# A hybrid decoder layer on one core: DeltaNet keys transposed on TensorE instead of through VectorE and DRAM, norm factors stored by GpSimd, head 0's values turned later

## The chip, the cores and the metric

The kernel runs on one core of a Trainium2 chip. The metric is the device time of one execution in microseconds, taken as the median of several executions. A profile is a record of one execution; it names TensorE as PE (its weight loads as PEld), VectorE as DVE, ScalarE as ACT, GpSimd as POOL and SyncE, which issues DMAs, as SP.

## The reference

Two decoder layers on 512 tokens of 1024 columns, float32. Each layer runs two branches side by side on the same normalised input, merges them with gates, projects the result, and adds a feed-forward block. What the change touches is the DeltaNet branch with its 8 heads of 128 columns, cut to its core:

```python
q, k, v, z, beta, decay = parts of  rmsnorm(x) @ w_in
q, k, v = silu(causal_conv4(q | k | v));  q, k = l2norm(q) * 128**-0.5, l2norm(k)
# per head, in chunks, with g the running sum of log decay in a chunk:
L      = strict_lower((k * beta) @ k.T * decay)           # I + L is inverted against
u, w   = solve(I + L, v * beta),  solve(I + L, k * beta * exp(g))
for each chunk, with a state S of 128 x 128:
    v_new = u - w @ S
    o     = (q * exp(g)) @ S + (q @ k.T * decay) @ v_new
    S     = S * exp(g_last) + (k * exp(g_last - g)).T @ v_new
o = rmsnorm(o, norm_g) * silu(z)                          # per head and token
```

The layer then forms sigmoid(gate_a) * (o @ w_up_dn) + sigmoid(gate_b) * (swa @ w_up_sw), projects it with w_o, and adds the feed-forward block. swa is a sliding-window attention with sinks.

## The kernel before, in words

**Tiling.** Activations lie with columns on the 128 partitions and the 512 tokens along the free side. A float32 matmul is made of three faster ones on high and low halves, so a projection of 128 columns (`mm_a`) is 8 x 3 = 24 matmuls of 128x128 by 128x512. Weights come in as `wr`, ScalarE makes the high half `wh`, VectorE the low half `wl`. The chunk of the delta rule is 128 tokens here, so a head has 4 chunks (`NC`).

**Stages of a layer.** First norm and projections, mixed with the sliding-window attention. There the keys of all heads are made and stored to DRAM (`kkd`), as are the decay matrices (`dd`), and a triangular solve (`solve`) prepares blocks of the inverse. Then a loop over eight blocks (`ps_us`, m = 0..7) up-projects the attention branch; ahead of it `d_dense(0)` makes head 0's values, queries and gate. Then the DeltaNet stage, a loop over 8 heads. In head h it calls, in this order:

- `d_keys(h + 1)`: loads `D` and `kk`, forms the factor `kds`, and makes `kd`, the keys with tokens on the partitions, times that factor;
- `d_inverse(h)`: three levels of the block inverse for heads h .. h + 3 (`ps_i` on TensorE, small copies on VectorE; on GpSimd a MEMSET and copies into `Pt`, then two copies into `T`);
- `d_chain(h)`: `ps_qk` and `aT`, then per chunk `ps_ks`, `rr`, `ps_y`, `yy`, `ps_su`, the state `St`, and `ps_o`; each step waits for the one before it, and what is left of TensorE is filled with the projections of the next head;
- `d_step`: one step of the norm of a finished head (`d_tail`, three steps that are spread over later heads). The sums of squares go to DRAM as a row (`sd`), come back as 128x4 (`ff`), GpSimd raises them to the power −1/2, they go to DRAM again (`fd`) and come back on all partitions (`fb`), and VectorE multiplies `yf` with them;
- `d_dense(h + 1)`: the projections `ps_vp`, `ps_qp`, `ps_zp` of the next head, 24 matmuls each, with a convolution of three VectorE operations on values and on queries.

After the last head come the remaining gate projections (`ps_ga`), `yT` (the halves of `yf`), the up-projection `ps_ud`, w_o and the feed-forward block.

**How keys and values get their tokens onto the partitions.** `by_token` does both. VectorE transposes 32x32 blocks of a 128x512 tile (STREAM_TRANSPOSE), four DMAs store the result to DRAM with the blocks in their new places (`kxd` or `vxd`), and one DMA loads it back (second half of the tile `kx` or `vx`). Keys of all heads share one tile `kx`, values one tile `vx`. ScalarE then makes four scaled copies of 128x128 each (`kd`, `vs`).

**What sets the order.** The program text gives priorities; a scheduler then lays out each engine's instructions in one fixed queue, and each engine works through its queue in order, waiting where an input is late. All dynamic DMAs are issued by SP, in its own order. PSUM banks come from pools: two for projections (`PM`), three for the chain (`PS`), one for `ps_i` (`PK`), and two (`PZ`, tag "ss") for a second `ps_i` tile and `ps_o`.

Of the kernel before, what the change touches and what calls it, by code (L numbers as in the profile page):

```python
# [10 lines left out]
F32 = mybir.dt.float32  # L11
# [3 lines left out]
AF = mybir.ActivationFunctionType  # L15
# [5 lines left out]
P = 128  # L21
# [4 lines left out]
H = 8  # L26
# [93 lines left out]
def hybrid_trunk(ctx, tc, x, positions, pre_mix_g, dn_conv_w, dn_a_log, dn_dt_bias, dn_norm_g,  # L120
# [15 lines left out]
    act, stt = nc.scalar.activation, nc.vector.scalar_tensor_tensor  # L136
    tt, ts = nc.vector.tensor_tensor, nc.vector.tensor_scalar
    ptt = nc.gpsimd.tensor_tensor
    dma = nc.sync.dma_start

    def pool_of(tag, bufs):
        def get(name, dt=F32, n=512):
# [112 lines left out]
    pd = dr.tile([P, 1024], F32, name="pd")  # L255
    dd = dr.tile([H, P, 512], F32, name="dd")
    kkd = dr.tile([H, P, 512], F32, name="kkd")
    kxd = dr.tile([H, P, 512], F32, name="kxd")
    vxd = dr.tile([H, P, 512], F32, name="vxd")
    gd = dr.tile([32, P], F32, name="gd")  # L260
    sd = dr.tile([H, 512], F32, name="sd")
# [258 lines left out]
    for l in range(depth):  # L520
# [460 lines left out]
        dn = {}  # L981

        urs = [X4("ur") for i in range(2)]
        kx, vx = X4("kx"), X4("vx")
        uview = lambda h: c4(urs[h // 2 % 2][:, h % 2 * 512:(h % 2 + 1) * 512])
        lo_, hi_ = slice(0, 64), slice(64, 128)
        r0, r1, r2, r3 = (slice(b * 32, (b + 1) * 32) for b in range(4))
# [68 lines left out]
                    ts(out=c4(Pt)[ra, :, rb], in0=v4(psq[ra, 256:384]), scalar1=-1.0, scalar2=None,  # L1056
                       op0=ALU.mult)

        def by_token(src, x_, via):


            a_, b_ = x_[:, 0:512], x_[:, 512:1024]
            nc.vector.transpose(a_.rearrange("p (b c i) -> p b c i", b=4, c=NC),
                                src.rearrange("p (c b j) -> p b c j", b=4, c=NC))
            for a in range(4):
                dma(via[:, a * P:(a + 1) * P].rearrange("(b j) f -> j b f", b=4),
                    a_[a * 32:(a + 1) * 32, :].rearrange("j (b f) -> j b f", b=4))
            dma(b_, via)
            return b_.rearrange("p (a c i) -> p a c i", a=4, c=NC)

        def d_keys(h):

            d, k_ = T[3]("D"), T[3]("kk")
            dma(d, dd[h])
            dma(k_, kkd[h])
            kds = sm.tile([P, NC], F32, name="kds")
            tc.keep_in_program_order(tt(out=kds, in0=cj[h], in1=c4(d)[:, :, P - 1], op=ALU.mult))
            kt = by_token(k_, kx, kxd[h])
            kd = T[7]("kd")
            for c in range(NC):  # L1080
                act(out=kd[:, c * P:(c + 1) * P].rearrange("p (a i) -> p a i", a=4), in_=kt[:, :, c, :],
                    func=AF.Copy, scale=kds[:, c:c + 1])
            dn["k", h] = d, k_, kd

        def d_dense(h, after=lambda: None):
            egb = T[6]("egb")
            dma(c4(egb), egd[h * NC:(h + 1) * NC, :].partition_broadcast(P))
            ps = PM("ps_vp")
            mm_a(ps, hT)
            vt = by_token(conv_silu(ps, 16 + h, T[5], "vv"), vx, vxd[h])  # L1090
            after()
            ps = PM("ps_qp")
            mm_a(ps, hT)
            qq = conv_silu(ps, h, T[4], "qq")
            after()
            ps = PM("ps_zp")
            mm_a(ps, hT)
            sz = T[6]("sz")
            act(out=sz, in_=ps, func=AF.Tanh, scale=0.5)
            stt(out=sz, in0=sz, scalar=1.0, in1=ps, op0=ALU.add, op1=ALU.mult)  # L1100
            after()
            d_step(h - 2)
            qe = T[7]("qe")
            ptt(out=qe, in0=qq, in1=egb, op=ALU.mult)

            wq = T[4]("wq")
            act(out=wq, in_=qq, func=AF.Square, scale=(EPS * P) ** 0.5)
            dn["d", h] = qq, qe, wq, vt, sz

        yf = []  # L1110

        def d_tail(h):

            w, y1 = dn.pop(("t", h))
            wh, wl = pair(T[5], "w")
            split(w, wh, wl)
            ps = PS("ps_w")
            mm(ps, lhsT=ones_r, rhs=wh, start=True, stop=False)
            mm(ps, lhsT=ones_r, rhs=wl, start=False, stop=True)
            nc.scalar.copy(w[0:1], ps[0:1])  # L1120
            dma(sd[h:h + 1, :], w[0:1])
            yield
            ff = sm.tile([P, NC], F32, name="ff")
            dma(ff, sd[h, :].rearrange("(p j) -> p j", p=P))
            ptt(out=ff, in0=ff, in1=mhalf, op=ALU.pow)
            dma(fd[h, :].rearrange("(p j) -> p j", p=P), ff)
            yield
            fb = T[6]("fb")
            dma(fb, fd[h, :].partition_broadcast(P))
            tt(out=y1, in0=y1, in1=fb, op=ALU.mult)  # L1130
# [8 lines left out]
        def d_chain(h):  # L1139
            Pt = dn.pop(("p", h))  # L1140
            d, k_, kd = dn.pop(("k", h))
            qq, qe, wq, vt, sz = dn.pop(("d", h))
            ps = PS("ps_qk")
            for c in range(NC):
                sl = slice(c * P, (c + 1) * P)
# [5 lines left out]
                    op0=ALU.mult, op1=ALU.mult)  # L1151
            vs = US("vs")
            for c in range(NC):
                act(out=vs[:, c * P:(c + 1) * P].rearrange("p (a i) -> p a i", a=4), in_=vt[:, :, c, :],
                    func=AF.Copy, scale=irk[h][:, c:c + 1])
            po = PZ("ps_o")
            St = None
            for c in range(NC):
# [35 lines left out]
        for t in range(NT):  # L1194
            tsl = slice(t * P, (t + 1) * P)
            for g in range(2):
                for j in range(g * 4, g * 4 + 4):
                    hi, lo = oT[j]
                    split(qt[t][:, j * P:(j + 1) * P], hi[:, tsl], lo[:, tsl])
        d_dense(0, lambda: steps(2))  # L1200
        for m in range(KT):
            ps = PM("ps_us")
            mm_a(ps, oT)
            mb = T[7]("mb")
            stt(out=mb, in0=sgb[m], scalar=1.0, in1=ps, op0=ALU.add, op1=ALU.mult)
            dma(mbd[m], mb)
            steps(2 if m < 6 else 40)
        for m in range(NA, NA2):
            ga_early(m)

# [238 lines left out]
```

## Time and profile before

| | us |
|---|---|
| median of 3 executions | 1840.2 (1839.76 to 1841.08) |
| the profiled execution's own time | 1841.73 |
| its span from first to last instruction | 1839.7 |
| TensorE busy | 1811.6 |
| VectorE busy | 1297.1 |
| ScalarE busy | 942.2 |
| GpSimd busy | 211.3 |

The mean granted clock of TensorE is 0.998 of full speed. The DeltaNet stage lies at about 291 to 490 us (layer 0) and 1198 to 1414 us (layer 1) of the span.

A row of the time line reads: start, duration, engine, line of the kernel, operation, output tile, inputs, shapes, count, and in brackets the time that the engine stood idle before it and what ended that. Two matmuls overlap: the second starts before the first has drained, so the time that a matmul costs TensorE is read from one start to the next (0.23 us between full ones), not from its duration (0.39). The same line numbers are used in the whole text; they are those of the kernel before, and in the pieces of the changed order those of the changed kernel, which differ by a few.

A row of the view by stretches reads: from:to in us, length, then busy us and instructions of PE, PEld, DVE, ACT and POOL, the granted clock of TensorE as a share, the share of the DMA engines, and GB/s.

### The profile page before, as it was taken

The page shows a single profiled execution, that of the slowest core. Times are in us where ns is not written, and L with a number is a line of the kernel's source. Part 1 is how long each engine was busy: PE and PEld are TensorE (multiplying, and loading weights), DVE is VectorE, ACT ScalarE, POOL GpSimd, SP SyncE. Part 2 cuts the span into 40 slices and gives each one's busy share as a digit, 9 for nine tenths or more (in the row PEclk, how much of TensorE's full clock was granted, in tenths as well). Part 3 has the DMA queues.
Part 4 walks back from the last instruction along what each step waited for, and adds up shares of the span by engine and source line. Part 5 has one row for each costly group of instructions (what it writes and reads, how often), then busy time and mean ns, then how long its engine had stood idle before and what let it go on. Part 6 is the DMA issues. An engine that isn't in the chain of part 4 may idle for free.

```text
span 1839.7 us, 26716 instructions
## 1 busy us (share of the span) xinstructions
PE 1811.6 (98%) x9598; PEld 1504.2 (82%) x9598; DVE 1297.1 (71%) x2466; ACT 942.2 (51%) x1913; POOL 211.3 (11%) x370
## 2 busy tenths in 40 slices
PE   9999999999999999999999999999999999999998
PEld 7888788778788888888898887887787888888886
DVE  5499796888566668684556987878784667585934
ACT  6678743444334645554347877234343346554542
POOL 0322101221101000000013231022111010000000
PEclk9999999999999999999999999999999999999999
DMA  5533447565453263464245333575555533544631
GB/s 187 201 117 117 115 134 228 159 172 162 118 200 126 92 217 121 167 218 149 93 155 179 113 118 104 172 212 160 151 160 155 170 116 124 185 153 152 229 107 46
DMA packets 148214, 278.48 MB, mean 151 GB/s; under 512 B 35361, under 2 KB 68449, under 8 KB 148082
## 3 DMA queue, kind: packets, MB, share of 16 engines
q1 hardware_dynamic: 148082, 276.79, 47.0%
q8 instruction: 75, 1.23, 0.3%
q14 instruction: 57, 0.47, 0.1%
HBM read 239.38 MB, written 37.36 MB: 150 GB/s over the span
## 4 chain that ended last, share of the span: by engine, by line
PE 79%; DVE 7%; ACT 5%; DMA 4%; issue 3%; POOL 1%; SPq 0%; POOLq 0%; DVEq 0%; ACTq 0%
PE ps_f L340 6%; PE ps_f L339 6%; PE ps_f L341 5%; PE ps_p L402 4%; PE ps_p L404 3%; PE ps_p L400 3%; PE ps_b L388 3%; PE ps_b L387 3%; PE ps_b L389 2%; PE ps_us L339 2%; PE ps_us L340 2%; PE ps_us L341 2%; PE ps_qp L340 2%; PE ps_qp L341 1%; PE ps_qp L339 1%
## 5 line engine op out<-in xcount | busy, mean ns | idle before, releaser
L323 ACT CAST wh<-wr 128x1024 fp32r<-128x1024 f32 (+1 forms) x332 | 343.4, 1040 | 557.6 <-PE ps_f L340 145.9
L324 DVE TENSOR_TENSOR wl<-wr,wh 128x1024 fp32r<-128x1024 f32 (+1 forms) x332 | 398.8, 1211 | 304.7 <-ACT wh L323 301.3
L339 PE MATMUL ps_f<-g_h,wh 128*128 128x512 f32 x448 | 174.3, 389 | 0.0
L340 PE MATMUL ps_f<-g_l,wh 128*128 128x512 f32 x448 | 174.3, 389 | 0.0
L341 PE MATMUL ps_f<-g_h,wl 128*128 128x512 f32 x448 | 174.3, 389 | 0.0
L402 PE MATMUL ps_p<-wl,P_h 128*128 128x512 f32 x336 | 131.3, 391 | 0.8 <-DVE wl L324 0.8
L404 PE MATMUL ps_p<-wh,P_l 128*128 128x512 f32 x336 | 130.8, 389 | 0.0
L400 PE MATMUL ps_p<-wh,P_h 128*128 128x512 f32 x336 | 129.5, 389 | 0.0
L437 POOL TENSOR_TENSOR pr<-pq,pw 128x1 f32<-128x1 f32 x16 | 9.7, 608 | 804.1 <-DVE pq L436 804.1
L341 PEld LDWEIGHTS ps_f<-g_h,wl 128*128 128x128 f32 x448 | 84.1, 188 | 17.5
L339 PEld LDWEIGHTS ps_f<-g_h,wh 128*128 128x128 f32 x448 | 84.1, 188 | 17.5
L340 PEld LDWEIGHTS ps_f<-g_l,wh 128*128 128x128 f32 x448 | 84.1, 188 | 17.2
L402 PEld LDWEIGHTS ps_p<-wl,P_h 128*128 128x128 f32 x336 | 63.1, 188 | 15.5 <-DVE wl L324 2.2
L400 PEld LDWEIGHTS ps_p<-wh,P_h 128*128 128x128 f32 x336 | 63.1, 188 | 13.3
L404 PEld LDWEIGHTS ps_p<-wh,P_l 128*128 128x128 f32 x336 | 63.1, 188 | 12.8
L387 PE MATMUL ps_b<-wh,h_h 128*128 128x432 f32 (+1 forms) x192 | 71.1, 370 | 0.0
L388 PE MATMUL ps_b<-wl,h_h 128*128 128x432 f32 (+1 forms) x192 | 70.6, 368 | 0.2 <-DVE wl L324 0.2
L389 PE MATMUL ps_b<-wh,h_l 128*128 128x432 f32 (+1 forms) x192 | 70.3, 366 | 0.0
L293 DVE TENSOR_TENSOR wr<-wr 128x1024 f32<-128x1024 f32 x48 | 57.9, 1219 | 2.5 <-DMA wr<-in_weights_dram 1.9
L339 PE MATMUL ps_qp<-h_h,wh 128*128 128x512 f32 x128 | 54.2, 424 | 0.0
L341 PE MATMUL ps_qp<-h_h,wl 128*128 128x512 f32 x128 | 53.4, 417 | 0.0
L340 PE MATMUL ps_qp<-h_l,wh 128*128 128x512 f32 x128 | 53.2, 416 | 0.0
(358 smaller groups left out, 4874.3 us busy)
## 6 DMA issues: line engine op xcount, KB each, us to landing
wr<-in_weights_dram SPq DMA_DIRECT2D x320, 512.0 KB, 4.1
wr<-in_weights_dram SPq DMA_DIRECT2D x24, 432.0 KB, 4.1
D<-dd SPq DMA_DIRECT2D x32, 256.0 KB, 3.8
xd<-xo SPq DMA_DIRECT2D x12, 512.0 KB, 2.6
xt<-xd SPq DMA_DIRECT2D x24, 256.0 KB, 3.5
D<-gd SPq DMA_DIRECT2D x16, 256.0 KB, 5.7
dd<-D SPq DMA_DIRECT2D x16, 256.0 KB, 2.8
kkd<-kk SPq DMA_DIRECT2D x16, 256.0 KB, 2.0
```

The costliest lines, as they stand in the source:

```text
L293: tt(out=held[j], in0=held[j], in1=part(i, k, j), op=ALU.add)
L323: nc.scalar.copy(wh[:, :w], wr[:, :w])
L324: sub(out=wl[:, :w], in0=wr[:, :w], in1=wh[:, :w].bitcast(F32), op=ALU.subtract)
L339: mm(ps, lhsT=wh[:, k, :], rhs=hi, start=k == 0, stop=False)
L340: mm(ps, lhsT=wh[:, k, :], rhs=lo, start=False, stop=False)
L341: mm(ps, lhsT=wl[:, k, :], rhs=hi, start=False, stop=k == KT - 1)
L387: mm(pss[t], lhsT=hi[:, tsl], rhs=wh[:, r, :], start=k == 0, stop=False)
L388: mm(pss[t], lhsT=hi[:, tsl], rhs=wl[:, r, :], start=False, stop=False)
L389: mm(pss[t], lhsT=lo[:, tsl], rhs=wh[:, r, :], start=False, stop=k == KT - 1)
L400: mm(pss[t], lhsT=hi[:, c], rhs=wh[:, r, :], start=first, stop=False, skip_group_check=onto)
L402: mm(pss[t], lhsT=hi[:, c], rhs=wl[:, r, :], start=False, stop=False, skip_group_check=onto)
L404: mm(pss[t], lhsT=lo[:, c], rhs=wh[:, r, :], start=False, stop=last, skip_group_check=onto)
```

## The change

Three edits.

1. Keys: `d_keys` no longer calls `by_token`. Four 128x128 transposes on TensorE (`tr`, a matmul with the identity) write the head's keys into a PSUM bank of `PZ` (`ps_kt`), and ScalarE's four scaled copies read that bank. The tile `kx`, the DRAM buffer `kxd`, one VectorE transpose, four stores and one load per head are gone.
2. Factors: the store `fd` is issued by GpSimd (`pdma`) instead of SP.
3. Values of head 0: `d_dense` returns the turn of its values as a function. For the other heads it is called at once, as before; for head 0 it is called after block m = 1 of the `ps_us` loop.

The diff, without lines that only rename or reflow:

```diff
-    dma = nc.sync.dma_start
+    dma, pdma = nc.sync.dma_start, nc.gpsimd.dma_start
...
-    kxd = dr.tile([H, P, 512], F32, name="kxd")
...
-        kx, vx = X4("kx"), X4("vx")
+        vx = X4("vx")
...
-        def by_token(src, x_, via):
-            a_, b_ = x_[:, 0:512], x_[:, 512:1024]
+        def by_token(src, b_, via):
+            a_ = vx[:, 0:512]
...
-            kt = by_token(k_, kx, kxd[h])
+            ps = PZ("ps_kt")
+            for c in range(NC):
+                sl = slice(c * P, (c + 1) * P)
+                tr(ps[:, sl], k_[:, sl], ident)
             kd = T[7]("kd")
             for c in range(NC):
-                act(out=kd[:, c * P:(c + 1) * P].rearrange("p (a i) -> p a i", a=4), in_=kt[:, :, c, :],
-                    func=AF.Copy, scale=kds[:, c:c + 1])
+                sl = slice(c * P, (c + 1) * P)
+                act(out=kd[:, sl], in_=ps[:, sl], func=AF.Copy, scale=kds[:, c:c + 1])
...
-            vt = by_token(conv_silu(ps, 16 + h, T[5], "vv"), vx, vxd[h])
+            vv = conv_silu(ps, 16 + h, T[5], "vv")
+            turn = lambda: dn.update({("v", h): by_token(vv, vx[:, 512:1024], vxd[h])})
+            if h > 0:
+                turn()
...
-            dma(fd[h, :].rearrange("(p j) -> p j", p=P), ff)
+            pdma(fd[h, :].rearrange("(p j) -> p j", p=P), ff)
...
-        d_dense(0, lambda: steps(2))
+        turn0 = d_dense(0, lambda: steps(2))
...
             steps(2 if m < 6 else 40)
+            if m == 1:
+                turn0()
```

The scheduler lays out the engines' queues anew, so instructions move that no line of the diff names. Three places matter for what follows.

GpSimd, in the turn of head h = 4 of layer 0 (the factors are those of head 2), before (`Pt` and `T` are copies of `d_inverse`, `ff` and `qe` as above):

```order
L1048 MEMSET Pt 128x512
L1050 COPY Pt<-Pc 32x4x32 x4
L1052 COPY T_96<-Tc 32x4x32 x2
L1125 TENSOR_TENSOR ff<-ff,pw 128x4
L1104 TENSOR_TENSOR qe<-qq,egb 128x512
```

The same place in the changed kernel:

```order
L1047 MEMSET Pt 128x512
L1049 COPY Pt<-Pc 32x4x32 x4
L1131 TENSOR_TENSOR ff<-ff,pw 128x4
L1132 DMA fd<-ff 128x4
L1109 TENSOR_TENSOR qe<-qq,egb 128x512
L1051 COPY T_96<-Tc 32x4x32 x2
```

The power `ff` moved from behind the copies `T` to ahead of them, the store `fd` came onto this queue right behind it, and `T` went behind `qe`. In the changed kernel the order is this one in the other turns too.

TensorE, at the end of a head's gate projection, before:

```order
L339 MATMUL ps_zp<-h_h,wh 128x512
L340 MATMUL ps_zp<-h_l,wh 128x512
L341 MATMUL ps_zp<-h_h,wl 128x512
L1013 MATMUL ps_i<-T_96,ur 64x64
L1015 MATMUL ps_i<-Pt,z_4109 64x64
```

and in the changed kernel:

```order
L338 MATMUL ps_zp<-h_h,wh 128x512
L339 MATMUL ps_zp<-h_l,wh 128x512
L340 MATMUL ps_zp<-h_h,wl 128x512
L1080 MATMUL ps_kt<-ident,kk 128x128 x4
L1012 MATMUL ps_i<-T_96,ur 64x64
L1014 MATMUL ps_i<-Pt,z_4103 64x64
```

The four transposes of the next head's keys stand between the last projection and the block inverse. Behind the inverse, `ps_qk` stood amid the value projection before, and stands directly behind `ps_i` in the changed kernel in 12 of 16 heads (of the two pieces here the first is of before, the second of the change):

```order
L340 MATMUL ps_vp<-h_l,wh 128x512
L1146 MATMUL ps_qk<-qq,kk 128x128 x4
L341 MATMUL ps_vp<-h_h,wl 128x512
```

```order
L1028 MATMUL ps_i<-Pc,z_4105 32x32
L1152 MATMUL ps_qk<-qq,kk 128x128 x4
L338 MATMUL ps_vp<-h_h,wh 128x512
```

Ten heads moved in this way. In the tail of layer 1, 33 instead of 28 matmuls `ps_ga` stand between the last `ps_o` and the first `ps_ud`.

VectorE, between two heads, before (the `714` lines are the convolution of the queries, `wl` the low halves of weights):

```order
L714 SCALAR_TENSOR_TENSOR qq<-ps_qp,cw,qq 128x509
L324 TENSOR_TENSOR wl<-wr,wh 128x1024
L714 SCALAR_TENSOR_TENSOR qq<-ps_qp,cw,qq 128x510
L1063 STREAM_TRANSPOSE kx<-kk 128x512
L714 SCALAR_TENSOR_TENSOR qq<-ps_qp,cw,qq 128x511
L412 TENSOR_TENSOR w_l<-w,w_h 128x512
L324 TENSOR_TENSOR wl<-wr,wh 128x1024
L718 SCALAR_TENSOR_TENSOR qq<-th,qq 128x512
L1100 SCALAR_TENSOR_TENSOR sz<-sz,ps_zp 128x512
L1077 TENSOR_TENSOR kds<-cj,D 128x4
```

and in the changed kernel:

```order
L323 TENSOR_TENSOR wl<-wr,wh 128x1024
L713 SCALAR_TENSOR_TENSOR qq<-ps_qp,cw,qq 128x509
L411 TENSOR_TENSOR w_l<-w,w_h 128x512
L713 SCALAR_TENSOR_TENSOR qq<-ps_qp,cw,qq 128x510
L713 SCALAR_TENSOR_TENSOR qq<-ps_qp,cw,qq 128x511
L717 SCALAR_TENSOR_TENSOR qq<-th,qq 128x512
L1105 SCALAR_TENSOR_TENSOR sz<-sz,ps_zp 128x512
L1076 TENSOR_TENSOR kds<-cj,D 128x4
L323 TENSOR_TENSOR wl<-wr,wh 128x1024
```

The transpose is gone, the split `w_l` (the sums of squares on their way to `sd`) stands earlier, and a weight conversion went from ahead of `kds` to behind it.

SP issues 96 DMAs fewer: 64 stores `kxd`, 16 loads `kx`, and the 16 stores `fd` that GpSimd issues now. The load `fb` stands behind fewer issues.

More of the change, by code (lines that the diff above doesn't have):

```diff
@@ L1107, in d_dense @@
             act(out=wq, in_=qq, func=AF.Square, scale=(EPS * P) ** 0.5)
-            dn["d", h] = qq, qe, wq, vt, sz
+            dn["d", h] = qq, qe, wq, sz
+            return turn
         yf = []
@@ L1141, in d_chain @@
             d, k_, kd = dn.pop(("k", h))
-            qq, qe, wq, vt, sz = dn.pop(("d", h))
+            (qq, qe, wq, sz), vt = dn.pop(("d", h)), dn.pop(("v", h))
             ps = PS("ps_qk")
@@ L1153, in d_chain @@
             for c in range(NC):
-                act(out=vs[:, c * P:(c + 1) * P].rearrange("p (a i) -> p a i", a=4), in_=vt[:, :, c, :],
-                    func=AF.Copy, scale=irk[h][:, c:c + 1])
+                act(out=vs[:, c * P:(c + 1) * P].rearrange("p (a i) -> p a i", a=4),
+                    in_=vt[:, :, c, :], func=AF.Copy, scale=irk[h][:, c:c + 1])
             po = PZ("ps_o")
```

## The prediction

> **What bounds the kernel now.** The first view is the page with its busy shares and the chain that ended last; the next is the busy time of each engine in stretches of the time line, for the two stretches in which the DeltaNet heads run.
>
> ```profile
> span 1839.7 us, 26716 instructions
> PE 1811.6 (98%) x9598; PEld 1504.2 (82%) x9598; DVE 1297.1 (71%) x2466; ACT 942.2 (51%) x1913; POOL 211.3 (11%) x370
> PE 79%; DVE 7%; ACT 5%; DMA 4%; issue 3%; POOL 1%; SPq 0%; POOLq 0%; DVEq 0%; ACTq 0%
> ...
> 291.00:490.00 199.00, 195.70 (x1407) 158.22 (x1406) 156.10 (x313) 86.25 (x163) 38.35 (x65) 1.00 0.55 163
> 1198.00:1414.00 216.00, 210.83 (x1466) 170.54 (x1466) 162.77 (x320) 90.61 (x169) 42.32 (x69) 0.99 0.55 163
> ```
>
> TensorE works for 1811.6 of 1839.7 us, so at most 28 us can be won without taking work from it. The edits all lie in the two DeltaNet stretches, where it stands still for 3.3 us (199.00 − 195.70) and 5.2 us. VectorE is 78% and 75% busy there. The change therefore adds to the engine that sets the time and relieves one that sets it only where a wait says so. The third view, the waits of TensorE, tells where that is:
>
> ```profile
> PE ps_y L1170 <- DVE rr L1167: 3.6, 2, 2.1
> PE ps_su L1175 <- DVE yy L1172: 3.0, 7, 0.6
> PE ps_ud L340 <- DVE yT_l L412: 1.7, 2, 1.4
> ```
>
> Columns are us in total, times and the longest. All three end on VectorE: two long waits for `rr`, seven short ones for `yy`, two at the tail for `yT_l`. They are what can be won; the transposes are what is paid.
>
> **Part 1: 64 transposes on TensorE.** Sixteen groups of four 128x128 transposes are added, 8 heads by 2 layers. The kernel already has such groups in its attention part, amid 128x512 matmuls:
>
> ```profile
> L922 PE MATMUL ps_pt<-ident,M x128: 270/272/333, 89.5 to 1143.5; 128*128 128x128 f32 x128
> ...
> 113.81 0.40 PE L341 MATMUL ps_kp<-h_h,wl 128*128 128x512 f32 x1
> 114.04 0.60 PE L922 MATMUL ps_pt<-ident,M 128*128 128x128 f32 x4
> 114.40 0.48 PE L339 MATMUL ps_kp<-h_h,wh 128*128 128x512 f32 x1
> 114.71 0.39 PE L340 MATMUL ps_kp<-h_l,wh 128*128 128x512 f32 x1
> ...
> 423.65 0.39 PE L341 MATMUL ps_zp<-h_h,wl 128*128 128x512 f32 x1
> 423.97 0.27 PE L1013 MATMUL ps_i<-T,ur 64*64 64x64 f32 x1
> ```
>
> Matmuls overlap, so starts are compared, not durations. From 113.81 to 114.71 is 0.90 us. Without the group it would be two steps of 0.23 (113.81 to 114.04 is one). The group costs 0.44, and 16 of them 7.0 us. From the second pair, the step from a wide matmul to a small one takes 0.32 instead of 0.23, which is 0.09 for a change of shape. The order shows that `ps_qk` now stands directly behind `ps_i` instead of amid `ps_vp`, in ten of the 16 heads, which saves one such step each: 0.9. Net **+6.1**. Bounds: the four starts alone (114.04 to 114.40, 0.36 x 16 = 5.8, less 0.9: 4.9) and no saving (7.0). The price by own duration, 64 x 0.272 = 17.4, is a rival below.
>
> **Part 2: the norm factors.** In the turn of head 4 (of 0 to 7) of each layer TensorE stands still for `rr`. Read from the last row backwards:
>
> ```profile
> 396.19 0.38 SPq L1124 DMA_DIRECT2D ff<-sd  x1
> 399.82 1.59 POOL L1052 COPY T<-Tc 32x128 f32<-32x128 f32 x2 [4.16 <-PE ps_i L1013]
> 401.49 1.33 POOL L1125 TENSOR_TENSOR ff<-ff,pw 128x4 f32<-128x4 f32 x1
> 402.85 0.34 SPq L1126 DMA_DIRECT2D fd<-ff  x1
> 404.73 0.39 SPq L1129 DMA_DIRECT2D fb<-fd  x1
> 408.53 0.40 PE L339 MATMUL ps_qp<-h_h,wh 128*128 128x512 f32 x1
> 409.46 0.69 DVE L1130 TENSOR_TENSOR yf<-yf,fb 128x512 f32<-128x512 f32 x1 [2.27 <-DMA fb<-fd]
> 410.47 0.49 PE L1170 MATMUL ps_y<-rr,Pt 128*128 128x128 f32 x2 [1.55 <-DVE rr L1167]
> ...
> 1317.13 0.40 PE L339 MATMUL ps_qp<-h_h,wh 128*128 128x512 f32 x1
> 1319.59 0.49 PE L1170 MATMUL ps_y<-rr,Pt 128*128 128x128 f32 x2 [2.07 <-DVE rr L1167]
> ...
> 1320.00:1322.00 2.00, 2.00 (x7) 1.52 (x6) 1.52 (x3) 1.28 (x4) 0.00 (x0) 0.50 0.90 355
> 1322.00:1330.00 8.00, 8.00 (x44) 6.79 (x43) 4.98 (x11) 2.25 (x5) 0.00 (x0) 0.91 0.35 114
> ```
>
> `rr` stands behind `yf` on VectorE; `yf` waits 2.27 us for `fb`; `fb` follows `fd`; `fd` waits for GpSimd's `ff`; and `ff` is queued on GpSimd behind the copies `T`, which had waited 4.16 us for `ps_i`. In this turn alone `ff` stands behind `T`; in the changed order it stands ahead of it in every turn, and its store right behind it on the same queue. Then `ff` waits only for its own input, whose load was issued at 396.19. In the head quoted below that takes 1.8 us (371.18 to 372.95), so `ff` could start at 398.0, 3.5 us earlier, against 2.27 us that are missing. TensorE's loss is 410.47 − 408.53 = 1.94 less 0.23 = 1.7 in layer 0, and 2.46 − 0.23 = 2.2 in layer 1. In layer 1 the granted clock then falls to 0.50 for 2 us and stands at 0.91 over the next 8: (1 − 0.50) x 2 + (1 − 0.91) x 8 = 1.7, of which I take 1.6. Together **−5.5**.
>
> The new path, a store issued by GpSimd, is in no row of this kernel: the page shows all dynamic DMA on one hardware queue. Its bounds come from a head in which `yf` does not wait today:
>
> ```profile
> 371.18 0.34 SPq L1124 DMA_DIRECT2D ff<-sd  x1
> 372.95 1.07 POOL L1125 TENSOR_TENSOR ff<-ff,pw 128x4 f32<-128x4 f32 x1 [2.62 <-DMA ff<-sd]
> 374.10 0.43 SPq L1126 DMA_DIRECT2D fd<-ff  x1
> 378.51 0.34 SPq L1129 DMA_DIRECT2D fb<-fd  x1
> 383.06 0.68 DVE L1130 TENSOR_TENSOR yf<-yf,fb 128x512 f32<-128x512 f32 x1
> ```
>
> Here 4.4 us pass from `fd` to `fb`; in the turn of head 4 it was 1.9 (402.85 to 404.73). `fb` landed 4.7 us after its issue there (404.73 to 409.46), and in this row `yf` starts 4.55 after it: there is next to no slack, so today's cover is a store that takes up to 4.4 us. If GpSimd's store takes 1.9 nothing waits and `fb` is 2.5 early; at 4.4 nothing changes; only beyond that does `yf` wait in the ordinary heads. I take a value between the two rows, hence no cost. The 80 issues that leave SP (64 `kxd`, 16 `kx`) cannot make it worse.
>
> The Trainium skill speaks against this edit. Its page "SBUF — State Buffer", section "SBUF: two separate sides", says that a DMA from the GpSimd queue has its descriptors written by GpSimd's own cores and that these are locked out while VectorE runs an operation that takes the shared port pair. "DMA: Bandwidth & Descriptors", section "Specifications", gives such a DMA about 1 us to its first byte against about 0.6. By these the store would be late by an estimated 0.4 us, and by more beside a long VectorE operation; no run here shows it yet, and what it would cost is the second rival.
>
> On GpSimd itself the issue stands ahead of `qe` and `T`. Bounds are an SP issue (0.34) and a whole small operation (`ff`, 1.33). `qe` is first read after the first `yy`, several us later, and `T` by the next head's `ps_i`: nothing on the path.
>
> **Part 3: VectorE loses 16 transposes.**
>
> ```profile
> L1063 DVE STREAM_TRANSPOSE kx<-kk x16: 696/702/715, 297.2 to 1356.3; 128x512 f32<-128x512 f32 x16
> ...
> 382.35 0.39 PE L339 MATMUL ps_vp<-h_h,wh 128*128 128x512 f32 x1
> 382.86 0.28 DVE L1172 COPY yy<-ps_y 128x128 f32<-128x128 f32 x1
> 383.19 0.49 PE L1175 MATMUL ps_su<-yy,kd 128*128 128x128 f32 x2 [0.46 <-DVE yy L1172]
> ```
>
> The wait for `yy` costs 382.35 to 383.19, 0.84, less 0.23: 0.6 us; with five of seven times such a value, and two nearer 0.47, about 4.1 in all. VectorE works from the last head's `yf` to that `yy` with next to no pause, and 0.70 of it, `kx`, goes away. Against that, TensorE has the four transposes (+0.4) ahead of `ps_i` but reaches `ps_y` one `ps_qk` step earlier; its cover changes little. 0.7 is a little over the 0.6 that is missing, but the `wl` conversions move by whole operations of 1.2 us and may stand ahead instead. Bounds 0 and −4.1; I take the middle, **−2.0**. ScalarE's 64 scaled copies stay, read from PSUM instead of SBUF; ScalarE is 43% busy in the stretch and `kd` is read after `yy`: nothing.
>
> **Part 4: the ends of the stage.**
>
> ```profile
> 1410.44 1.07 PE L339 MATMUL ps_ud<-yT_h,wh 128*128 128x512 f32 x4
> 1412.87 0.50 PE L340 MATMUL ps_ud<-yT_l,wh 128*128 128x512 f32 x1 [1.36 <-DVE yT_l L412]
> ...
> 309.09 1.28 ACT L1081 ACTIVATE kd<-kx,kds 128x128 f32<-128x128 f32 x4 [4.82 <-DVE kds L1077]
> ```
>
> In the tail 33 instead of 28 `ps_ga` matmuls stand between the last `ps_o` and `ps_ud`. That is 5 x 0.23 = 1.1 us more cover where 1.4 is missing in layer 1 and 0.3 (1.7 − 1.4) in layer 0: **−1.4**. Bounds 0 and −1.7. At the start, the first `kd` waits 4.82 us for its factor; today it holds nothing, but now it empties a bank of the two that the transposes, `ps_i` and `ps_o` share, so the second head's transposes may wait for it. It is some 0.3 a layer (one 0.32 copy of the four): **+0.6**, bounds 0 and 1.3 (the whole copy) a layer. Head 0's values leave the early part for a loop in which VectorE is not late; left at nothing.
>
> **The sum.** +6.1 − 5.5 − 2.0 − 1.4 + 0.6 = −2.2 us. The profiled execution took 1841.73 (its span and 2.0 around it), 1.5 above the median of the three runs, 1840.2. Applied to it the sum gives 1839.5, and for the median **1838.0**.
>
> **The rivals.**
>
> *All waits go* (faster). If `yy` loses its whole 4.1, the tail 1.7, the start costs nothing and a group 0.36: 4.9 − 5.5 − 4.1 − 1.7 = −6.4, 1833.8. For it: the 0.7 is larger than each miss but one. Against: every wait that ends uncovers the next one.
>
> *GpSimd's store is late* (slower). In about 12 ordinary heads `yf` would wait for `fb`, with `St` and `rr` of the chain behind it on VectorE. Head 4's turn shows the exchange: 2.27 us of wait cost TensorE 1.7, so the first 0.6 is free. If the store takes 4.4 + 1.6 us, each costs 1.0: +12, and the two turns with the long waits keep 1.0 of them each, +2: −2.2 + 12 + 2 = +12, 1852. It makes the kernel slower by over 0.2% from −2.2 + 14 x = 3.7, x = 0.4: from 1.0 us later than today's 4.4, 5.4 us in all. Against: GpSimd is 20% busy in the stage, and 5.4 us is nearly three times the best row. This is the case of the rule above.
>
> *The transposes cost their own duration* (slower): 17.4 instead of 7.0, +10.4, 1848.4. Against: the group row at 114.04 has four in 0.60 us.
>
> *The reordering doesn't reach the wait*: `ff` goes first but the wait stays, because `fb` is held by something else: −2.2 + 5.5 = +3.3, 1843.5. Against: SP issued `fb` 1.9 us behind `fd`, with nothing else between but issues.
>
> **How the numbers follow.** A measurement of this kernel can tell about 0.2%, 3.7 us, from no change: faster is below 1836.5, slower above 1843.9. Likeliest case 0.50 (own range 1835 to 1841, with 0.10 below 1836.5), all waits go 0.24, the late store 0.12, own duration 0.04, no reach 0.10 (half of it slower). That gives faster 0.34, slower 0.12 + 0.04 + 0.05 = 0.21, same 0.45. The range reaches 1.3 under the best case, holds the case without reach, and leaves out the two dear ones: 1832.5 to 1844.5.
>
> **What would show it.** Step 1: 64 more transposes on TensorE, each group taking 0.4 us between starts, busy time up by about 6. Step 2: no `yf` row with a wait for `fb` over 1 us inside the heads, no granted clock of 0.50 there; `fd` to `fb` under 4.4 us. Step 3: fewer `ps_su` waits for `yy`. Step 4: `ps_ud` waits under 0.5. The prediction is wrong if the `yf` waits spread over the heads, if the wait moves to `ps_kt` for its PSUM bank or for `kk`, or if a group of transposes costs over 0.6 us.

## The result and the profile after

The changed kernel took 1846.39 us (median of 8, 1844.48 to 1847.42), the kernel before 1840.64 (median of 8): a ratio of 1.0032, 95% interval 1.0021 to 1.0043. It is 5.8 us **slower**; the forecast was 1838.0 in a range of 1832.5 to 1844.5. The profiled execution took 1846.94 us. First the page of the changed kernel, with its DMA queues:

```profile
span 1845.2 us, 26688 instructions
PE 1819.7 (99%) x9662; PEld 1509.2 (82%) x9662; DVE 1290.7 (70%) x2450; ACT 940.7 (51%) x1913; POOL 220.5 (12%) x386
q0 software_dynamic: 512, 0.03, 0.0%
```

The span grew by 5.5 us. TensorE's busy time grew by 8.1 (1811.6 to 1819.7), its idle time fell by 2.6 (28.1 to 25.5). So work was added and fewer waits were won than it costs. The queue q0 is new: GpSimd's 16 stores. The waits of TensorE in the changed kernel:

```profile
PE ps_su L1181 <- DVE yy L1178: 2.3, 10, 0.3
PE ps_ud L339 <- DVE yT_l L411: 2.1, 3, 1.0
PE ps_y L1176 <- ACT vs L1160: 1.3, 2, 0.7
PE ps_ks L1170 <- DVE St L1184: 1.2, 1, 1.2
```

The two long waits for `rr`, 3.6 us before, are gone. But the waits for `yy` are ten instead of seven, with 2.3 instead of 3.0 us; the tail's wait for `yT_l` grew from 1.7 to 2.1; and two waits are new, for `vs` on ScalarE and for `St` on VectorE. The time line of the changed kernel, the turn of head 4 in layer 0:

```profile
398.54 1.04 POOL L1131 TENSOR_TENSOR ff<-ff,pw 128x4 f32<-128x4 f32 x1 [4.05 <-DMA ff<-sd]
399.87 0.62 POOL L1132 DMA_DIRECT2D fd<-ff  x1 [0.29 <-POOL ff L1131]
401.96 0.44 SPq L1135 DMA_DIRECT2D fb<-fd  x1
407.78 0.69 DVE L1136 TENSOR_TENSOR yf<-yf,fb 128x512 f32<-128x512 f32 x1 [0.32 <-DMA fb<-fd]
...
399.90 0.39 PE L339 MATMUL ps_zp<-h_l,wh 128*128 128x512 f32 x1
400.12 0.39 PE L340 MATMUL ps_zp<-h_h,wl 128*128 128x512 f32 x1
400.35 0.60 PE L1080 MATMUL ps_kt<-ident,kk 128*128 128x128 f32 x4
400.88 0.27 PE L1012 MATMUL ps_i<-T,ur 64*64 64x64 f32 x1
```

`ff` starts at 398.5 instead of 401.5, and `yf` waits 0.32 us instead of 2.27. The store by GpSimd is issued 0.29 us behind `ff` and takes 0.62 to issue (SP: 0.34, right behind `ff`); `fb` follows it by 2.1 us, much as in the best turn before (1.9). The group of transposes costs 400.12 to 400.88, 0.76, where the step from `ps_zp` to `ps_i` was 0.32: 0.44, as forecast. The tail of layer 0, where the last head's factor comes back:

```profile
490.09 0.58 ACT L1193 ACTIVATE w<-ps_o 128x512 f32<-128x512 f32 x1
499.01 0.42 SPq L1254 DMA_DIRECT2D mbr<-mbd  x1
499.53 0.38 SPq L1130 DMA_DIRECT2D ff<-sd  x1
506.04 1.03 POOL L1131 TENSOR_TENSOR ff<-ff,pw 128x4 f32<-128x4 f32 x1 [10.00 <-DMA ff<-sd]
507.36 0.59 POOL L1132 DMA_DIRECT2D fd<-ff  x1 [0.29 <-POOL ff L1131]
509.96 0.32 SPq L1135 DMA_DIRECT2D fb<-fd  x1
514.82 0.69 DVE L1136 TENSOR_TENSOR yf<-yf,fb 128x512 f32<-128x512 f32 x1 [9.91 <-DMA fb<-fd]
516.46 0.50 PE L339 MATMUL ps_ud<-yT_l,wh 128*128 128x512 f32 x1 [0.96 <-DVE yT_l L411]
```

and the same chain in the kernel before:

```profile
486.82 0.58 ACT L1187 ACTIVATE w<-ps_o 128x512 f32<-128x512 f32 x1
508.54 0.69 DVE L1130 TENSOR_TENSOR yf<-yf,fb 128x512 f32<-128x512 f32 x1 [7.61 <-DMA fb<-fd]
```

From the squares of the last `ps_o` to `yf` it is 24.7 us in the changed kernel and 21.7 before; in layer 1 it is 24.1 and 22.9. Here nothing lies between the factor and the matmul that needs it except a fixed stock of other matmuls (the cover of the tail), so every microsecond of this chain beyond the stock is TensorE's.

### The profile page after: what moved, and what is told of

Its sections match the earlier page's. It is cut to its first block, busy times and chain, and to the rows that moved or that the text cites. A ratio compares the mean times of both kernels' runs of the same rounds, so it can differ in the third digit from the quotient of the medians.

```text
span 1845.2 us, 26688 instructions
## 1 busy us (share of the span) xinstructions
PE 1819.7 (99%) x9662; PEld 1509.2 (82%) x9662; DVE 1290.7 (70%) x2450; ACT 940.7 (51%) x1913; POOL 220.5 (12%) x386
## 4 chain that ended last, share of the span: by engine, by line
PE 82%; DVE 7%; ACT 4%; DMA 3%; issue 1%; POOL 1%; SPq 0%; DVEq 0%; POOLq 0%; ACTq 0%
PE ps_f L338 6%; PE ps_f L339 6%; PE ps_f L340 5%; PE ps_p L401 4%; PE ps_p L399 4%; PE ps_p L403 4%; PE ps_b L386 3%; PE ps_b L387 3%; PE ps_b L388 3%; PE ps_us L338 2%; PE ps_us L340 2%; PE ps_us L339 2%; PE ps_qp L339 1%; PE ps_qp L338 1%; PE ps_qp L340 1%; DVE wl L323 1%
## 5 line engine op out<-in xcount | busy, mean ns | idle before, releaser
L399 PEld LDWEIGHTS ps_p<-wh,P_h 128*128 128x128 f32 x336 | 63.1, 188 | 13.5 <-ACT wh L322 0.2
L338 PE MATMUL ps_vp<-h_h,wh 128*128 128x512 f32 x128 | 53.8, 420 | 0.0
L909 ACT ACTIVATE M<-M,nm 128x128 f32<-128x128 f32 x128 | 49.8, 391 | 5.8 <-DVE nm L904 5.8
```

Of the source, the lines that this page charges most:

```text
L338: mm(ps, lhsT=wh[:, k, :], rhs=hi, start=k == 0, stop=False)
L399: mm(pss[t], lhsT=hi[:, c], rhs=wh[:, r, :], start=first, stop=False, skip_group_check=onto)
```

## The experiments

Two theories at the start. **A**: the transposes cost about 7 us and pay for an `rr` wait that came from the order of `ff` and `T` alone; the other two edits do nothing. **B**: GpSimd's store is what costs. All ratios below are to the kernel before, run on the same chip beside each group; 0.001 is 1.84 us.

### Each edit alone

**The wait for `rr`.** The kernel before, with one dependency that puts the two copies `T` behind `ff` in GpSimd's order. Only those rows of that one queue change, once a layer.

```diff
             ptt(out=ff, in0=ff, in1=mhalf, op=ALU.pow)
+            ffs[h] = nc.cur_bb.bb.instructions[-1]
...
                     nc.gpsimd.tensor_copy(T6v[r, :, r], Tcv[r, ah, :])
+                    if h - 2 in ffs:
+                        tc.add_manual_dep(nc.cur_bb.bb.instructions[-1], ffs[h - 2].name, ...)
```

> The kernel before, in which only GpSimd's queue is changed: in the turn of head 4 of each layer ff stands ahead of the copies T, as in the changed kernel; every other queue is as before. Theory A (the wait for rr came from that order alone, and the transposes paid for its removal): the two rr waits of 1.7 and 2.2 us and the slow clock behind the second (1.6) are gone, about 5.5 us faster than before, 1835.1. Rival (the wait went for another reason, the missing kxd transfers or GpSimd's store): the yf wait stays near 2.3 us and the time stays at 1840.6.

Measured: 1838.78 us, ratio 0.9980 (0.9971 to 0.9988), 3.7 us faster than before. Its waits:

```profile
PE ps_ud L340 <- DVE yT_l L412: 3.2, 2, 1.9
PE ps_su L1179 <- DVE yy L1176: 3.2, 7, 0.6
PE ps_y L1174 <- DVE rr L1171: 0.8, 1, 0.8
```

The order alone removes most of the wait, without a transpose and without GpSimd's store. 0.8 us of it stay, and the tail's wait grows from 1.7 to 3.2: of the forecast 5.5, about 2.3 are left behind or given back, and 3.7 arrive.

**The keys alone**, with `fd` on SP and head 0's values at their old place; and **keys and late values**, with `fd` on SP, run twice:

```diff
-            pdma(fd[h, :].rearrange("(p j) -> p j", p=P), ff)
+            dma(fd[h, :].rearrange("(p j) -> p j", p=P), ff)
```

and, for the keys alone, head 0's values turned where they were:

```diff
-            if h > 0:
-                turn()
+            turn()
...
-            if m == 1:
-                turn0()
```

> The changed kernel with only its first edit: keys by TensorE, fd stored by SP, head 0's values at their old place. Theory A: 64 transposes cost about 7.3 us of TensorE time, the other two edits next to nothing: 1846 within 1.5 us, like the whole change. Rival B (the store by GpSimd is what costs): 1843 or less, at least 3 us below the whole change.

> The changed kernel with fd stored by SP again; keys and head 0's values as in the change. Theory A: within 1.5 us of the whole change, 1846.4. Rival B: at least 3 us less. If it differs from the run with the keys alone by over 1.5 us, the late values of head 0 have a price of their own.

> The changed kernel with fd stored by SP once more, beside the two runs with a covered tail. If GpSimd's store costs about 4.8 us in the changed kernel (1.0032 twice with it, 1.0006 without), it comes again at 1.000 to 1.0015. If it was chance, near 1.003.

Measured: keys alone 1.0006 (0.9997 to 1.0014); keys and values 1.0006 (0.9998 to 1.0015) and 1.0000 (0.9991 to 1.0009). The late values of head 0 do nothing that these intervals show. Theory A fell in its second half: without GpSimd's store the change costs nothing that can be told from no change, and with it 0.0032. The changed kernel itself, run again beside other variants, says that this is no accident of one chip:

> The changed kernel once more, as it is, beside the variants of this group. If the ratio of 1.0032 is its own and not that of one chip, it comes again within 0.001: between 1.0022 and 1.0042. If GpSimd's store costs nothing and the two runs without it (1.0006 both) were only taken beside a slower kernel before, it comes out near 1.0006 here.

Measured: 1.0032 (1.0019 to 1.0044). So **moving the store to GpSimd costs 0.0026 to 0.0032 in this kernel, about 5 us**; the intervals leave 2 to 3 us either way, and the five profiled executions differ by 3.3 us on average. Between the changed kernel and the one with keys and late values, 4 matmuls of TensorE and 8 operations of VectorE stand at other places in their queues, and on SP, beside the 16 stores, some 18 other DMAs. These 18 all lie in the two tails.

**The store alone**, on the kernel before:

```diff
-            dma(fd[h, :].rearrange("(p j) -> p j", p=P), ff)
+            pdma(fd[h, :].rearrange("(p j) -> p j", p=P), ff)
```

> The kernel before with only the second edit: fd stored by GpSimd. In the order that the scheduler then makes, ff stands behind the copies T in the turns of heads 3 and 4 of each layer, not in that of head 4 alone. Theory D (the store costs at the tail, the order of ff and T sets the rr wait): two long yf waits per layer instead of one and a tail 1 us later per layer, 5 to 7 us slower than before, ratio 1.003 to 1.004. Rival (the store by GpSimd is harmless, what costs in the changed kernel is its combination with the transposes): 1.000.

Measured: 1865.02 us, ratio **1.0120** (1.0106 to 1.0134), 22 us slower; both sides of the expectation were far off (it counted two turns with `ff` behind `T`, there are three). Its waits, the time line of the turn of head 4 of layer 0, and the stretch behind it:

```profile
PE ps_y L1170 <- DVE rr L1167: 14.0, 6, 3.2
PE ps_su L1175 <- DVE yy L1172: 6.6, 7, 1.9
```

```profile
401.12 1.59 POOL L1052 COPY T<-Tc 32x128 f32<-32x128 f32 x2 [3.85 <-PE ps_i L1013]
402.79 1.37 POOL L1125 TENSOR_TENSOR ff<-ff,pw 128x4 f32<-128x4 f32 x1
404.45 0.62 POOL L1126 DMA_DIRECT2D fd<-ff  x1 [0.29 <-POOL ff L1125]
411.97 0.69 DVE L1130 TENSOR_TENSOR yf<-yf,fb 128x512 f32<-128x512 f32 x1 [3.51 <-DMA fb<-fd]
412.98 0.49 PE L1170 MATMUL ps_y<-rr,Pt 128*128 128x128 f32 x2 [3.25 <-DVE rr L1167]
```

```profile
413.00:425.00 12.00, 12.00 (x58) 10.21 (x59) 8.52 (x16) 4.96 (x10) 0.00 (x0) 0.86 0.38 120
```

With the store on GpSimd's queue the scheduler puts `ff` and `fd` behind `T` in three turns of each layer (heads 3, 4 and 5) instead of one. It is the chain of the prediction, three times. In the turns of heads 3 and 4 it ends in a wait for `rr`, in that of head 5 in one for `yy` (1.8 and 1.9 us); the other two `rr` waits come in the last head's turn. Four of the eight gaps over 1.5 us are followed by a stretch of slow clock, 0.86 over 12 us as here; behind the other four the clock stood at 1.00. To see how much of the 22 us is order, only GpSimd's queue was changed again, with `ff` and its store ahead of `T` in every turn (12 rows; the other queues row for row as in the run with the store alone):

> The run with GpSimd's store alone (1.012), with GpSimd's queue changed and nothing else: in every turn ff and its store stand ahead of the copies T. Theory D (the 22 us came from ff standing behind T in three turns a layer): the rr waits of 14 us and the slow clock behind them go, about 18 to 20 us, and what stays is the store's own price at the tail, 2 to 5 us over the run with ff first and SP's store (0.998): ratio 0.999 to 1.001. Rival (the store itself is slow in every turn): the yf waits stay and the ratio stays above 1.006.

Measured: 1.0050 (1.0037 to 1.0064). The order accounts for 13 of the 22 us. What stays, 9 us over before and 13 over its twin with SP's store (`ff` first, 0.998), is more than theory D had. In its profile `rr` still waits 8.7 us, in five places. The rows put that delay ahead of the store: for four of the factors 1 to 5 of each layer `ff` starts 3.4 to 3.8 us behind the issue of its load, for the fifth 1.8; in the twin two of five are that late. From `fd` to `fb` it is no longer (1.8 to 3.8 us, in the twin 1.9 to 4.5). The scheduler has also moved some 500 of TensorE's 9598 matmuls and 64 of SP's DMAs against that twin, so this remainder isn't the store's price alone, and no run here separates the two.

### Where the store costs

Theory **D**: at the end of the stage, where the last factors are waited for at once. Rival **E**: in every turn. First, the last three heads' stores went back to SP:

```diff
-            pdma(fd[h, :].rearrange("(p j) -> p j", p=P), ff)
+            (dma if h >= 5 else pdma)(fd[h, :].rearrange("(p j) -> p j", p=P), ff)
```

> The changed kernel with fd of the last three heads (5, 6, 7) stored by SP, the other five by GpSimd as in the change. Theory D (GpSimd's store costs only where a factor is waited for at once: the last head's turn and the tail behind it, where the changed kernel shows ps_ks +1.4 and ps_ud +1.6 and +0.8): near the runs with all stores on SP, ratio 1.0006 to 1.0014. Rival E (it costs in every turn, or through GpSimd's queue): at most three eighths of the difference is gained, 1.0022 or more.

Measured: 1.0012 (1.0003 to 1.0021), against 1.0032 in the same group. Three eighths of the stores carry 0.0020 (the two intervals leave 0.0015 either way) of the 0.0026 to 0.0032. Then a pair whose edits differ in the store alone, with 24 gate matmuls of each layer moved from ahead of the heads to behind them, as cover for the tail (work for TensorE while the last factors are on their way):

```diff
-NA2 = NA + 2
+NA2 = NA + 1
```

> The changed kernel with 24 matmuls ps_ga of each layer moved from ahead of the heads to behind them, 5.4 us more cover for the last two factors; GpSimd stores fd. Theory D (the store costs at the tail): the ps_ud waits of 3.2 us go and with them most of the store's price: 1.0032 falls to 1.0010, and to within 0.0007 of its twin with SP's store. Rival E (it costs in the turns of the heads): it falls by the tail's waits alone and stays 0.002 or more above its twin.

> The twin: the same cover at the tail, fd stored by SP. Its ps_ud waits were only about 1 us, so little goes: 1.0000 to 1.0006 by theory D and by rival E alike. What tells them apart is its distance from the run with GpSimd's store.

Measured: with GpSimd's store 1.0009 (1.0000 to 1.0018), with SP's 1.0003 (0.9995 to 1.0012). Under cover the distance is 0.0006 instead of some 0.003, and neither has a wait for `yT_l`. Rival E, which asked for 0.002 or more, falls. The traces without cover say the same. In the changed kernel and with SP's store (three runs) TensorE works through the same matmuls in the same order, but for four. From the first `ps_qk` of the last head to the first `ps_wo` behind the tail it took 91.0 and 88.6 us in layer 0 of the changed kernel (its two profiles) and 89.2 and 89.6 in layer 1, against 87.8 to 88.3 and 87.6 to 88.1 with SP's store. Over both layers that is 3.2 us on average, all but 0.1 of what the profiled executions differ by. So **moving the store costs in the last head's turn and in the tail**. Without cover, the waits of the run with keys and late values (second run) and then its tail of layer 0, to set beside those of the changed kernel:

```profile
PE ps_su L1181 <- DVE yy L1178: 2.4, 10, 0.3
PE ps_y L1176 <- ACT vs L1160: 1.3, 2, 0.7
PE ps_ud L339 <- DVE yT_l L411: 0.2, 1, 0.2
```

```profile
488.19 0.58 ACT L1193 ACTIVATE w<-ps_o 128x512 f32<-128x512 f32 x1
496.88 0.43 SPq L1130 DMA_DIRECT2D ff<-sd  x1
501.67 1.25 POOL L1131 TENSOR_TENSOR ff<-ff,pw 128x4 f32<-128x4 f32 x1 [8.47 <-DMA ff<-sd]
502.94 0.32 SPq L1132 DMA_DIRECT2D fd<-ff  x1
505.44 0.32 SPq L1135 DMA_DIRECT2D fb<-fd  x1
510.79 0.69 DVE L1136 TENSOR_TENSOR yf<-yf,fb 128x512 f32<-128x512 f32 x1 [8.14 <-DMA fb<-fd]
```

The waits for `yy` and `vs` are those of the changed kernel. The one for `yT_l` is 0.2 instead of 2.1; in the changed kernel's second profile it is 1.5, in the other two runs with SP's store 0.2 and 0.3. The one for `St` (1.2, the last head's turn) isn't there, but it belongs to one execution: the second profile of the changed kernel has 0.8 in another turn, and the first run with keys and late values 0.6.

From the squares to `yf` it is 22.6 us here, 24.7 with GpSimd's store; over both layers it is 23.8 to 24.7 in the two profiles of the changed kernel and 22.4 to 23.6 in the three with SP's store. Of the 2.1 us the store itself has 0.4: from the end of `ff` to `fb` 2.5 (502.92 to 505.44) against 2.9 (507.07 to 509.96). The greater part comes earlier in the chain: from the squares to `ff` 13.5 us here, 16.0 there. Some 0.7 comes back, as `ff` is shorter there and `fb` lands sooner.

`ff` waits for a load of 2 KB that stands among large loads of 256 KB (`mbr`, `sgr`), and SP issues these in another order. Here the load of `ff` stands right behind the `fb` of the head before, and three large loads follow it; then SP comes to `fd` and waits there for `ff`, so that the next large load goes out at 503.30. In the changed kernel an `mbr` stands ahead of the load of `ff` (499.01), which is issued 9.4 us behind the squares instead of 8.7. Six large loads follow it by 503.66, since no `fd` holds SP up. `ff` then starts 6.5 us behind the issue of its load instead of 4.8.

Under cover the two orders of SP are nearly alike, but for the stores. There `ff` starts 11.8 to 12.1 us behind the squares with either store, and the chain to `yf` is no longer with GpSimd's (19.5 and 19.9 us, against 20.7 and 21.4 with SP's). So the pair shows where the price is paid, not that the cover hides a longer chain. That the large loads make the small one late is an inference: no run changes SP's order alone, and in the run with the store alone, which has the order of the changed kernel here, `ff` starts 4.8 and 5.1 us behind its load.

### The price of the transposes, and the two new waits

Each transpose issued twice, into the same place:

```diff
                 tr(ps[:, sl], k_[:, sl], ident)
+                tr(ps[:, sl], k_[:, sl], ident)
```

> The changed kernel with each of the 64 transposes issued twice, into the same place. By the changed kernel's trace four in a row start 0.111 us apart, so 64 more add 7.1 us to TensorE. Theory A (TensorE is the bound, its added work goes to the end one to one): 1853.5, 7.1 over the changed kernel. Rival C (TensorE has slack there, the loss is in waits): under 3 us over it, below 1849.5. Own duration of a transpose, 0.27 us, would give 1863.

Measured: 1.0060 (1.0047 to 1.0072), 0.0028 or 5.2 us over the changed kernel; the two intervals leave some 3 us either way, and the scheduler moved some 600 other matmuls too. So the time is nearer to theory A, and doesn't shut out C alone. TensorE's busy time rose by 7.4 (1819.7 to 1827.1). The 64 of the change have a price of 7.2 us by the busy time of two runs without a long gap: 1811.4 (`ff` first) and 1818.6 (keys and values, second run).

The new waits, taken away at their source: `vs` is copied ahead of `kd` on ScalarE, and GpSimd loads `ff` itself. In the changed kernel that load stood behind four `vxd` stores on SP (before behind two), and in the last head's turn it was issued 2.9 us after `sd`:

```profile
465.89 0.26 SPq L1127 DMA_DIRECT2D sd<-w  x1
466.90 1.78 SPq L1065 DMA_DIRECT2D vxd<-vx  x4
468.79 0.39 SPq L1130 DMA_DIRECT2D ff<-sd  x1
479.57 0.69 DVE L1136 TENSOR_TENSOR yf<-yf,fb 128x512 f32<-128x512 f32 x1 [1.76 <-DMA fb<-fd]
480.52 0.49 PE L1170 MATMUL ps_ks<-St,kk 128*128 128x128 f32 x2 [1.20 <-DVE St L1184]
```

```diff
-            dma(ff, sd[h, :].rearrange("(p j) -> p j", p=P))
+            pdma(ff, sd[h, :].rearrange("(p j) -> p j", p=P))
...
+            together = Order(nc.scalar)
+            together.begin()
             vs = US("vs")
...
+            dn.pop(("e", h + 1))()
+            together.end()
```

(`dn["e", h + 1]` holds the four copies `kd` of the next head, which `d_keys` now hands on instead of making them.)

The late load alone doesn't make the wait for `St`: with SP's store it is issued 2.9 us after `sd` as well, and nothing waits. What differs in this turn is the time from `fd` to `fb`, 3.4 us against 2.3; in the changed kernel's second profile it is 2.0, and there is no such wait.

> The changed kernel with its two new waits taken away at their source: ScalarE copies the values vs ahead of the next head's keys kd, and GpSimd loads ff itself, so that the load does not stand behind four value stores on SP. Theory A (these waits are on the path): 0.8 + 0.8 us for vs and up to 1.4 us for St come back, about 3 us below the changed kernel, ratio 1.0016. Rival (each is only moved on to the next wait, the tail above all): no gain, 1.003.

Measured: 1.0021 (1.0013 to 1.0030), 2 us below the changed kernel, which the two intervals (some 3 us either way) don't tell from nothing. The wait for `vs` is gone and 0.2 us is left for `St`; the waits for `yy` grew from 2.3 to 3.2. Whether a part of the expected 3 us came stays open.

### The waits for `yy`

Here VectorE was to have 0.7 us less ahead of `yy` (`kx`), yet the waits stayed. One more weight conversion was taken out of VectorE's way in each turn: a dependency, for the order only, puts the first `wl` that `d_dense(h + 1)` asks for behind the first `yy` of head h (`gate`).

```diff
+            if gate:
+                tc.add_manual_dep(nc.cur_bb.bb.instructions[-1], gate.pop().name, ...)
```

(The lines that put the first `yy` of a head into `gate` are left out here.)

> The changed kernel with one weight conversion wl (1.2 us) of each turn held on VectorE until the first yy is copied; 10 of 14 turns then have one wl fewer ahead of yy. Theory G (the kx transposes' 0.7 us were not gained at yy because conversions stand ahead of it on VectorE): the ten ps_su waits for yy of 0.4 us go, about 4 us below the changed kernel, ratio 1.001. Rival (yy waits for something else, ps_qk or ps_i): the waits stay, 1.003.

Measured: 1.0051 (1.0036 to 1.0065). Theory G, that VectorE's load ahead of `yy` sets the wait, fell here: with one conversion of 1.2 us held back there are eleven waits of 4.4 us in all. The time line shows why. First the changed kernel, then this run, in the same turn:

```profile
405.96 0.38 PE L1176 MATMUL ps_y<-vs,Pt 128*128 128x128 f32 x2
406.14 1.13 DVE L1156 SCALAR_TENSOR_TENSOR aT<-ps_qk,cj,D 128x128 f32<-128x128 f32 x4
407.18 0.28 DVE L1178 COPY yy<-ps_y 128x128 f32<-128x128 f32 x1
407.51 0.49 PE L1181 MATMUL ps_su<-yy,kd 128*128 128x128 f32 x2 [0.23 <-DVE yy L1178]
```

```profile
405.23 0.38 PE L1179 MATMUL ps_y<-vs,Pt 128*128 128x128 f32 x2
405.57 1.12 DVE L1159 SCALAR_TENSOR_TENSOR aT<-ps_qk,cj,D 128x128 f32<-128x128 f32 x4
406.62 0.28 DVE L1181 COPY yy<-ps_y 128x128 f32<-128x128 f32 x1
406.95 0.49 PE L1186 MATMUL ps_su<-yy,kd 128*128 128x128 f32 x2 [0.41 <-DVE yy L1181]
```

Counted from the first `ps_qk` of the turn (401.98 and 402.38), `yy` did come 1.0 us earlier, but the scheduler had placed `ps_y` 1.1 us earlier on TensorE too. What was held back stood ahead of the four operations `aT`. These 1.1 us stand directly ahead of `yy` in both runs, and `yy` starts as they end, 1.2 and 1.4 us behind `ps_y`. TensorE has four `ps_vp` matmuls for that time in both; in the kernel before it has five in the turns of heads 1 to 4. What VectorE loses the scheduler uses to pull the waiting matmul forward, and the wait stays.

### A version that beats both

`ff` ahead of `T` on the kernel before, and the 24 gate matmuls moved to the tail; then the same with the hold on `wl`:

> The kernel before with ff ahead of T (the run at 0.998) and 24 matmuls ps_ga of each layer moved from ahead of the heads to behind them, so that 52 instead of 28 stand between the last ps_o and ps_ud: 5.4 us more cover for the last two factors. Theory F (the tail's wait for yT_l, 2.3 and 2.0 us in that run, is given back there by a chain of DRAM trips of fixed length): both go, 4 us below it, ratio 0.9957. Rival: the start of the heads, which loses these 24 matmuls as cover, waits as much: 0.998 or more.

> The fastest run so far (ff ahead of T, 24 ps_ga matmuls moved to the tail, 0.9975), with the same hold on one wl of each turn. Its profile shows nine ps_su waits for yy, 4.2 us. Theory G: most of them go, 3 to 4 us below it, ratio 0.9955. Rival: conversions held back make the next matmuls wait for wl, 0.9975 or more.

Measured: 0.9975 (0.9965 to 0.9984) and 0.9996 (0.9987 to 1.0004). The first is the fastest of all runs, 4.6 us below before. Its list has no wait for `yT_l`, but 4.2 us for `yy` and 1.7 for `rr`: the 5.4 us of cover brought about 1, less than the intervals tell from nothing. In the second the waits for `yy` fell by half, from 4.2 to 2.1 us, so there theory G had a part of the truth; but `rr` waits 4.2 us, and the gain is lost.

## Why the prediction was wrong, point by point

- **Part 1, the transposes: +6.1, measured 7.2.** A group costs 0.44 as worked out; the 0.9 that the new place of `ps_qk` was to save isn't seen in the busy time (in the other two runs with SP's store the price comes out at 7.5 and 7.8).
- **Part 2, the `rr` waits: −5.5.** The mechanism was right: both waits and the slow clock are gone, and `ff` ahead of `T` does it alone but for 0.8 us. The size was not: the tail gives 1.5 back, and 3.7 arrive when it is done alone.
- **Part 2, GpSimd's store: 0, measured about +5.** This step failed most. It has 5 of the 8 us between forecast and result; with the store on SP the same change comes out at 1.0000 to 1.0006, by these ratios about 1841 us, inside the range. The step weighed the store itself, in the ordinary turns, and there it was right: `fd` to `fb` takes 1.8 to 4.4 us in the changed kernel's two profiles, 2.8 and 2.6 on average, against 2.6 to 2.8 on average with SP's store. It did not weigh the last head's turn and the tail, for which the same part quoted no row of `fd`, though `ps_ud` stood among the waits; there the price lies. Nor did it ask what SP would do without `fd` in its queue. Of the 2.1 us more in the tail's chain the store has 0.4; most of the rest is the load of `ff`, which lands later while SP issues the large loads around it in another order. Why it lands later stays open. The rival *GpSimd's store is late* had the sign and the issuing engine, but put the price into 12 ordinary heads and asked for 1.0 us of lateness there. By the rule of the Trainium skill cited in the prediction ("SBUF — State Buffer", "SBUF: two separate sides") GpSimd could not write the store's descriptors while VectorE runs an operation that takes the shared port pair. The trace doesn't show such a delay: the store's issue takes 0.59 to 0.76 us and `fd` lands within the bounds.
- **Part 3, `yy`: −2.0, measured −0.7** (3.0 to 2.3 us of waits), and next to nothing counted as the prediction does, from start to start (4.1 to 4.0). The step took the place of `ps_su` on TensorE as given; the scheduler moved it with VectorE's queue.
- **Part 4, the tail: −1.4.** In place of it the wait grew by 0.4, because the chain to `yf` grew by 3.0 us in layer 0 and by 1.2 in layer 1, as much there as the 1.1 us of new cover. With SP's store the wait is 0.2 to 0.3, so this step failed only through the one on the store. **The start: +0.6** is in no wait of the list.
- **Not in the sum:** the waits for `vs` (1.3), from a queue laid out anew, `kd` ahead of `vs` on ScalarE; they are there with SP's store too. The wait for `St` (1.2) is in one of the two profiles alone.
- **The other rivals.** *All waits go* and *no reach* are out. *Own duration* is out: 0.44 a group, not 1.09.

## What to carry to other kernels

Price a changed DMA path at the place where its result is waited for at once, not where it has slack: here the heads hid the store by GpSimd and the tail did not. Look also at the queue that the store leaves: once `fd` was gone from SP, its large loads went out at other moments. Read a reordered queue for what stands ahead of a short operation at the head of a long chain: one pair of copies ahead of `ff` was worth 3.7 us in one turn of each layer and 13 us in three, and could be had with a dependency instead of 64 matmuls. And where a scheduler places the waiting instruction, work taken off the engine it waits for may only move it forward, as it did in one of two trials here.

## What was not expected of the hardware

A store of 2 KB issued by GpSimd started 0.29 us behind the operation before it and took 0.62 us to issue, against next to nothing and 0.32 to 0.34 on SP, and landed in about the same time (`fd` to `fb` above). Over a chain of three DRAM trips at the tail, however, its user came later by more than these differences explain: from the squares to `yf` 24.7 us against 22.6 in the two tails shown. That isn't a trait of the store alone: under cover the chain was shorter with GpSimd's store than with SP's (19.5 and 19.9 us against 20.7 and 21.4).

The clock didn't follow from the length of a gap alone. In the run with the store alone, gaps of 1.80 and 1.94 us were followed by a granted clock of 0.86 over 12 us, and gaps of 2.25 and 2.44 us by 1.00.
